# The chunked recurrence of one RWKV mixer: two summands stacked on the partitions, and Gram products with K and B as one weight

## The chip, the core and the metric

The kernel runs on one core of a Trainium2 chip. A core has engines that each work through a queue of their own in order: TensorE (PE in the profile; its weight loads are PEld) multiplies matrices into the accumulation memory PSUM, VectorE (DVE) and ScalarE (ACT) work on rows of 128 partitions, GpSimd (POOL) is a general engine, and SyncE (SP) issues the transfers (DMAs) between the off-chip memory and the on-chip buffer. Semaphores make an engine wait for another. The metric is the time of one execution on the chip in microseconds (us), less is better.

## The reference

The whole program is two transformer blocks over 1024 positions of width 1024. The change is inside the first block's RWKV branch. Per head (8 heads of 64) and direction (forward and reversed) it runs this recurrence over the 1024 positions:

```python
def step(state, inp):
    r_t, w_t, k_t, v_t, a_t, b_t = inp
    sa = jnp.einsum('bhvk,bhk->bhv', state, a_t)
    state = (state * w_t[:, :, None, :] + sa[..., None] * b_t[:, :, None, :]
             + v_t[..., None] * k_t[:, :, None, :])
    return state, jnp.einsum('bhvk,bhk->bhv', state, r_t)
y_f = wkv7_scan(r_h, decay_h[:, :, 0], k_dir[:, :, 0], v_h, -kk, kk * a_h[:, :, 0])
y_b = fl(wkv7_scan(fl(r_h), fl(decay_h[:, :, 1]), fl(k_dir[:, :, 1]), fl(v_h),
                   fl(-kk), fl(kk * a_h[:, :, 1])))
```

`w` (decay) and `a` come from small products of rank 64 (LORA). Beside it stands an attention branch (MLA, 8 heads); both are gated, multiplied by a branch matrix and by `w_out`, and go into a mixture of experts. The second block (windowed attention, a gated linear recurrence, experts) follows. Everything but the first block's mixer is left as it is.

## The kernel before

The recurrence is computed in chunks of CH = 64 positions (NCH = 16 of them) and in fp32, of which each matmul is two records of PE. A pair p of heads (four pairs) lies on the two halves of the 128 partitions, one head on each; both directions (u or d, 0 and 1) lie side by side in the columns.

`phase_a` makes the input projection z tile by tile (matmuls of three split terms, L286 to L288). Its hook `after` starts the RWKV work as the tiles of a pair are done. `prep` (four times for a pair: two halves g of the sequence, two directions d) makes, for eight chunks at once, the decayed keys K and B, the rows A and R (`rAR`), and from them by `gram` (L552) the four triangular 64x64 products of a chunk. There K and B are laid as block-diagonal weights (`diag`, L609 and L610) so that one matmul of 128 rows gives both heads. `flip` (L530) transposes four of the factors. All nine factors of a chunk go by DMA to `P.rw` in device memory, in one layout of 128 partitions. The LORA products at L580 contract over 64 rows, `twd` on one half of the partitions and `ad` on the other, so two of them can lie beside each other. `inverse` inverts the triangular matrices, on DVE for blocks of 32 (L655, L657) and with a few matmuls for the rest (L679, L683).

`rwkv_chain` then goes through the 16 chunks one after the other. For each chunk it has five steps, each a group of matmuls of 64x64 at L742 into the PSUM tile `pc` (two buffers): `ahead` (the two products for the next chunk that don't need the state, copied by ACT to `px`, L761), the main product (copied by DVE to `U`, L779), the state product (added by DVE to the decayed state `SW`, which POOL made at L775, into `S`, L788), and the output `Y` (copied by ACT, L792, and stored). In all it has nine terms for a direction and chunk: two in `ahead`, two in the main product, two for S, three for Y. The factors come back with one DMA for two chunks (`rwt`). `mm` issues the two halves (head 0, head 1) alternately, and an order on PE keeps one accumulation of a half at a time.

The chains of pairs 0 to 2 run inside the projection and the attention; chain 3 runs beside the end of the attention. Attention's steps on PE are scores (L286 to L288, tile `S<-kh,qh`), transposes (L900, `pt`), values (L914, `po`) and sums (L922). `finish` (L693 to L719) normalises a pair's output, and `branch_out` multiplies with the branch matrix (tile `br`), after splitting the inputs by ACT and DVE into two parts (L255: `wlo`, `ol`).

The order of instructions on an engine is no table: when the program is built, a scheduler goes through it with a cost model of its own and lays each engine's instructions in the order of the times that it estimates. So a changed step moves its neighbours, too.

## Time and profile before

| | us |
|---|---|
| median of the runs | 4181.69 (three runs, 4176.91 to 4192.26) |
| the profiled execution | 4153.57, span 4151.8 |
| PE busy | 3737.5 (90% of the span) |
| DVE busy | 2816.6 (68%) |
| ACT busy | 2112.2 (51%) |
| POOL busy | 417.2 (10%) |
| granted PE clock, mean over the span | 0.948 |

The span is the time from the first to the last instruction of the profiled execution. Busy time is the time in which an engine had an instruction at work. The granted clock is the share of full speed that PE was allowed. The rows below are of three kinds: a table of stretches of time with the busy time of each engine, a table of instructions grouped by line and shape, and a timeline of one engine, in which neighbours of one kind are merged.

### The profile page before, as it was taken

The numbers are of one execution on the slowest core, as the hardware profiler recorded it, in microseconds if no ns is written. First come the engines' busy times: TensorE is split into PE (matmuls) and PEld (weight loads), VectorE is DVE, ScalarE is ACT, GpSimd is POOL, SyncE is SP. The second block draws the span as 40 slices with busy tenths as digits, with TensorE's granted clock in tenths as the row PEclk, the third lists the DMA queues.
The fourth block names the chain that finished last, engine by engine and source line by source line (L and its number), as shares of the span: only waits on it lengthen the run. The fifth ranks groups of instructions, "written<-read, shape, count | busy, mean of one in ns | idle before, by whom it ended". The sixth has DMA issues, their size and how long they took to land. (4 is left out here: it accounts for less than half of the span.)

```text
span 4151.8 us, 57961 instructions
## 1 busy us (share of the span) xinstructions
PE 3737.5 (90%) x22538; PEld 2975.9 (72%) x22538; DVE 2816.6 (68%) x4374; ACT 2112.2 (51%) x2621; POOL 417.2 (10%) x313
## 2 busy tenths in 40 slices
PE   7999998999997979996999869999969986999994
PEld 6877776777675766664889757887748875788873
DVE  5556374958756556654366778888867766788887
ACT  4322323443332335554255546777738753677774
POOL 0000000100000014330000011111010000111101
PEclk9999998999998989998999989999979997999997
DMA  3355757563437569984233569999731355999994
GB/s 109 130 165 148 215 166 212 148 191 116 161 109 261 183 241 319 315 272 139 112 97 97 217 261 344 384 383 380 284 127 71 114 191 216 333 379 375 383 372 159
DMA packets 371044, 921.87 MB, mean 222 GB/s; under 512 B 156304, under 2 KB 214416, under 8 KB 298832
## 3 DMA queue, kind: packets, MB, share of 16 engines
q1 hardware_dynamic: 352336, 867.78, 57.9%
q0 software_dynamic: 18432, 50.36, 4.8%
q8 instruction: 178, 2.92, 0.3%
q14 instruction: 98, 0.80, 0.1%
HBM read 767.54 MB, written 167.25 MB: 225 GB/s over the span
## 5 line engine op out<-in xcount | busy, mean ns | idle before, releaser
L255 DVE TENSOR_TENSOR wlo<-wraw,whi 128x2048 fp32r<-128x2048 f32 x498 | 1134.1, 2289 | 297.9 <-ACT whi L255 295.3
L255 ACT ACTIVATE whi<-wraw 128x2048 fp32r<-128x2048 f32 x498 | 955.1, 1919 | 366.8 <-PE g L288 243.0
L287 PE MATMUL g<-wlo,xth 128*128 128x512 f32 x1280 | 509.2, 398 | 5.7 <-DVE wlo L255 5.6
L286 PE MATMUL g<-whi,xth 128*128 128x512 f32 x1280 | 511.4, 400 | 3.2 <-ACT xth L255 2.4
L288 PE MATMUL g<-whi,xtl 128*128 128x512 f32 x1280 | 506.8, 396 | 5.9 <-DVE xtl L255 5.6
L288 PEld LDWEIGHTS g<-whi,xtl 128*128 128x128 f32 x1280 | 242.6, 190 | 62.0 <-DVE xtl L255 10.6
L287 PEld LDWEIGHTS g<-wlo,xth 128*128 128x128 f32 x1280 | 243.1, 190 | 59.4 <-DVE wlo L255 7.9
L286 PEld LDWEIGHTS g<-whi,xth 128*128 128x128 f32 x1280 | 243.2, 190 | 57.3 <-ACT xth L255 4.8
L286 PE MATMUL z<-hT_hi,w_hi 128*128 128x512 f32 x592 | 240.8, 407 | 8.0 <-DVE z_out L402 6.4
L1646 POOL DMA_INDIRECT e_xg<-xm,e_ix x32 | 75.5, 2359 | 1711.2 <-DVE e_ix L1644 952.3
L287 PE MATMUL z<-hT_lo,w_hi 128*128 128x512 f32 x592 | 239.5, 404 | 0.0
L288 PE MATMUL z<-hT_hi,w_lo 128*128 128x512 f32 x592 | 238.3, 403 | 0.0
L287 PE MATMUL g<-wlo,e_hh 128*128 128x512 f32 x512 | 202.4, 398 | 15.2 <-DVE wlo L255 15.2
L286 PE MATMUL g<-whi,e_hh 128*128 128x512 f32 x512 | 204.4, 400 | 8.2 <-ACT e_hh L255 8.0
L288 PE MATMUL g<-whi,e_hl 128*128 128x512 f32 x512 | 196.5, 391 | 0.2
L775 POOL TENSOR_SCALAR SW<-S,wc 128x64 f32<-128x64 f32 x120 | 67.2, 575 | 773.6 <-DVE S L788 440.3
L286 PEld LDWEIGHTS z<-hT_hi,w_hi 128*128 128x128 f32 x592 | 113.3, 191 | 38.5 <-DVE z_out L402 6.6
L288 PEld LDWEIGHTS z<-hT_hi,w_lo 128*128 128x128 f32 x592 | 112.8, 191 | 31.6 <-issue 6.1
L287 PEld LDWEIGHTS z<-hT_lo,w_hi 128*128 128x128 f32 x592 | 113.5, 192 | 27.5 <-issue 2.3
L1246 PE MATMUL g<-wraw,m_hT 128*128 128x512 f32 x256 | 117.3, 598 | 13.6 <-ACT m_y L1247 6.8
L287 PEld LDWEIGHTS g<-wlo,e_hh 128*128 128x128 f32 x512 | 96.4, 188 | 42.9 <-DVE wlo L255 24.9
L286 PEld LDWEIGHTS g<-whi,e_hh 128*128 128x128 f32 x512 | 96.3, 188 | 32.9 <-ACT e_hh L255 14.4
(522 smaller groups left out, 8040.9 us busy)
## 6 DMA issues: line engine op xcount, KB each, us to landing
wraw<-in_w_gu SPq DMA_DIRECT2D x256, 1024.0 KB
wraw<-in_w_dn SPq DMA_DIRECT2D x128, 1024.0 KB
wraw<-in_w SPq DMA_DIRECT2D x96, 1024.0 KB
rwt<-rw SPq DMA_DIRECT2D x32, 1152.0 KB
w_raw<-in_w_in SPq DMA_DIRECT2D x37, 512.0 KB
rw<-flip SPq DMA_DIRECT2D x128, 128.0 KB
gt<-z_out SPq DMA_DIRECT2D x16, 512.0 KB
gate<-gt SPq DMA_DIRECT2D x32, 256.0 KB
```

Of the source, the lines that this page charges most:

```text
L255: return self.nc.scalar.activation(hi, src, AF.Copy), self.nc.vector.tensor_sub(lo, src, hi.bitcast(F32))
L286: t.matmul(ps, lh, rh, start=first, stop=False)
L287: t.matmul(ps, lh, rl, start=False, stop=False)
L288: t.matmul(ps, ll, rh, start=False, stop=last)
L775: nc.gpsimd.tensor_scalar(SW[:, d], S[:, d], P.wc[:, c, 4 * d + p:4 * d + p + 1], None, op0=OP.mult)
L1246: nc.tensor.matmul(ps, ht[:, k], w[:, k, n], start=(k == 0), stop=(k == 1))
L1646: nc.gpsimd.indirect_dma_start(out=xg, out_offset=None, in_=self.x, in_offset=bass.IndirectOffsetOnAxis(ap=ix[:, :1], axis=0))
```

## The change

Two factors whose products are summed anyway are laid above each other on the 128 partitions, so that one matmul of 128 rows makes the sum of both. To allow it, the chunk's tile in device memory gets a new layout (`RW` = 768 columns, `VU`, `XX`, `W2`, `W3`, `LL` and others are column offsets); U is written by the chain into the `rwt` tile under V, and `px`'s part into the tile under X. A chunk and direction has then six terms: two in `ahead` (64 rows), one main product (128 rows), one state product (128 rows), two for the output (one of 64 rows, one of 128). A head's results go to the other half of the partitions where that is needed.

```diff
@@ rwkv_chain
-    def parts(c):
-        if c % 2 == 0:
-            parts.R = pool.tile([128, 2, 1152], F32, name="rwt", bufs=2)
-            nc.sync.dma_start(parts.R, P.rw[p][c // 2])
+    def part(c):
+        R = pool.tile([128, 2, RW], F32, name="rwt", bufs=3)
+        for h, o in enumerate((AN, 0)):
+            nc.sync.dma_start(R[HALF[h], :, o:o + RW - AN], P.rw[p][c][HALF[h], :, o:o + RW - AN])
...
-        mm(ps, lambda u: [(LA[:, u], VT[:, u], 0)] + ([(AN[:, u], XT[:, u], 1)] if c else []))
-        t = pool.tile([128, 2, 2, CH], F32, name="px", bufs=2)
-        nc.scalar.activation(t[:, 0:n], ps[:, 0:128 * n].rearrange("p (x u t) -> p x u t", u=2, t=CH), AF.Copy)
+        t = [(la[h][HALF[h], u], vu[h][HALF[h], u], 1 - h, 64 * u) for u in U2 for h in range(2)]
+        if c:
+            t += [(an[HALF[1 - h], u], xx[h][HALF[1 - h], u], h, 128 + 64 * u) for u in U2 for h in range(2)]
+        mm(ps, t)
+        for h in range(2):
+            nc.scalar.activation(SP[HALF[1 - h], :, h], v(ps)[HALF[1 - h]], AF.Copy)
+            if c:
+                nc.scalar.activation(xx[h][HALF[h]], v(ps, 128)[HALF[h]], AF.Copy)
...
-            for d in U2:
-                nc.gpsimd.tensor_scalar(SW[:, d], S[:, d], P.wc[:, c, 4 * d + p:4 * d + p + 1], None, op0=OP.mult)
+            for h in range(2):
+                s = HALF[h]
+                nc.gpsimd.tensor_mul(SW[s], SP[s, :, h], P.wc[s, c, p:8:4][:, :, None].to_broadcast([64, 2, CH]))
-        mm(ps, lambda u: [(XT[:, u], px[:, 0, u], 0)] + ([(px[:, 1, u], S[:, u], 0)] if S is not None else []))
-        nc.vector.tensor_copy(Ut, v(ps))
+        mm(ps, [(xx[h][both[h], u], SP[both[h], u, h], 1 - h, 64 * u) for u in U2 for h in range(2)])
+        nc.vector.tensor_copy(vu[0][HALF[1]], v(ps)[HALF[1]])
+        nc.vector.tensor_copy(vu[1][HALF[0]], v(ps)[HALF[0]])
...
-            mm(ps, lambda u: [(KT[:, u], VT[:, u], 0), (BT[:, u], Ut[:, u], 0)])
+            mm(ps, [(w2[h][:, u], vu[h][:, u], h, 64 * u) for u in U2 for h in range(2)])
+            for h in range(2):
+                s = HALF[h]
+                if c:
+                    nc.vector.tensor_add(SPn[s, :, h], v(ps)[s], SW[s])
-                nc.vector.tensor_add(Sn, v(ps), SW)
...
-        mm(ps, lambda u: ([(S[:, u], Rr[:, u], 0)] if S is not None else [])
-           + [(VT[:, u], MK[:, u], 0), (Ut[:, u], MB[:, u], 0)])
+        t = [(SP[HALF[h], u, h], rr[HALF[h], u], h, 64 * u) for u in U2 for h in range(2)] if c else []
+        mm(ps, t + [(vu[h][:, u], w3[h][:, u], h, 64 * u) for u in U2 for h in range(2)])
```

In `prep` and `gram`, K and B of one head stand beside each other as one weight of 128 columns over that head's 64 rows. A matmul then gives all four blocks of one head, and the two heads use the two halves of the rows. All products of a group are masked on DVE. LORA products are cut into four of 128 columns, issued alternately.

```diff
@@ gram
-        for g in range(2):
-            ps = self.ps(0)
+        for q in range(2):
+            pm = [self.ps(0) for h in range(2)]
             for c in range(4):
-                nc.tensor.matmul(ps[:, 128 * c:128 * c + 128], lb[:, 4 * g + c], AR[:, :, 4 * g + c], start=True, stop=True)
-            if mask is None:
-                nc.scalar.activation(da[:, cs], v[:, :, 0], AF.Copy)
-            else:
-                nc.vector.tensor_mul(da[:, cs], v[:, :, 0], m(mask))
-            nc.vector.tensor_mul(dr[:, cs], v[:, :, 1], m("m_inc"))
+                for h in range(2):
+                    nc.tensor.matmul(pm[h][:, 128 * c:128 * c + 128],
+                                     KB[HALF[h], 4 * q + c].rearrange("p x t -> p (x t)"),
+                                     AR[HALF[h], :, 4 * q + c], start=True, stop=True)
+            for h in range(2):
+                v = pm[h].rearrange("p (c x t) -> p c x t", x=2, t=CH)
+                nc.vector.tensor_mul(lw[:, :, h], v[:, :, 0], m("m_str"))
+                nc.vector.tensor_mul(lw[:, :, 2 + h], v[:, :, 1], m("m_inc"))
@@ prep
-        for x, act in enumerate((P.twd, P.ad)):
-            nc.tensor.matmul(pm[x], up[rows[x], x], act[rows[x], ts], start=True, stop=True)
+        for q in range(4):
+            for x, act in enumerate((P.twd, P.ad)):
+                o = ts.start + 128 * q
+                nc.tensor.matmul(pm[x][:, 128 * q:128 * q + 128], up[rows[x], x], act[rows[x], o:o + 128],
+                                 start=True, stop=True)
```

The stores of the factors (`put`, `pairs`), the loads of `inverse` and the order of `flip`'s copies follow the new layout.

The scheduler lays the changed work anew. At three places it reads as follows. In the new kernel's listing the same steps have other line numbers: chain matmuls L759 (for L742), Gram products L555 (for L552), LORA products L585 (for L580), attention's transposes L926, values L940 and sums L948 (for L900, L914, L922), the U copies L801 and L802 (for L779), the state's additions L811 (for L788).

First, PE where attention ends and chain 3 goes on, before:

```order
L742 MATMUL pc<-rwt 64x64 x4
L900 MATMUL pt<-cst,p 128x128 x4
L914 MATMUL po<-pts,V 64x128 x8
L742 MATMUL pc<-rwt,U 64x64 x4
L914 MATMUL po<-pts,V 64x128 x7
L922 MATMUL po<-cst,m 64x128 x2
L695 MATMUL pc<-y_8353,cstb 128x512
```

And now:

```order
L940 MATMUL po<-pts,V 64x128 x7
L948 MATMUL po<-cst,m 64x128 x2
L759 MATMUL pc<-rwt 64x64 x4
L759 MATMUL pc<-rwt,SP 64x64 x4
L759 MATMUL pc<-rwt 64x64 x4
L514 MATMUL pc<-cst,hbc 128x128 x4
L759 MATMUL pc<-rwt 64x64 x8
L759 MATMUL pc<-SP,rwt 64x64 x4
L737 MATMUL pc<-r,cstb 128x512
L759 MATMUL pc<-rwt 64x64 x4
```

The last group of the chain stood ahead of attention's last; now eight more chunks stand behind it, 200 chain matmuls, with 30 matmuls of the branch product and some of `finish` among them.

Second, DVE at the same place, where before the last copies of the chain and of attention stood next to each other:

```order
L788 TENSOR_TENSOR S<-pc,SW 128x128
L926 TENSOR_TENSOR ot<-ot,po 128x128
L904 COPY pts<-pt 128x512
L779 COPY U<-pc 128x128
L926 TENSOR_TENSOR ot<-ot,po 128x128
```

And now:

```order
L801 COPY rwt<-pc 64x2x64
L802 COPY rwt<-pc 64x2x64
L811 TENSOR_TENSOR SP<-pc,SW 64x2x64 x2
L255 TENSOR_TENSOR wlo<-wraw,whi 128x2048
L801 COPY rwt<-pc 64x2x64
L802 COPY rwt<-pc 64x2x64
L255 TENSOR_TENSOR wlo<-wraw,whi 128x2048
L255 TENSOR_TENSOR ol<-oraw,oh 128x512 x3
L811 TENSOR_TENSOR SP<-pc,SW 64x2x64 x2
```

Each copy and each addition of a chunk is now two instructions on half of the partitions, and pieces of the branch product's split stand among them, which came behind the chain before.

Third, PE at the Gram products, where the number of the tile tells the half (a tile for each head, on its own half of the rows). Before, four of one tile on the whole array follow four of another:

```order
L552 MATMUL pw_1277<-rAR_1258,bd0_199 128x128 x4
L552 MATMUL pw_1284<-rAR_1258,bd0_199 128x128 x4
```

Now, in a place where they alternate, and in one where they don't:

```order
L555 MATMUL pw_1276<-rAR_1258,rKB_1266 128x128 x2
L555 MATMUL pw_1277<-rAR_1258,rKB_1266 128x128 x2
L555 MATMUL pw_1276<-rAR_1258,rKB_1266 128x128
L555 MATMUL pw_1277<-rAR_1258,rKB_1266 128x128
L555 MATMUL pw_1276<-rAR_1258,rKB_1266 128x128
L555 MATMUL pw_1277<-rAR_1258,rKB_1266 128x128
```

```order
L555 MATMUL pw_1530<-rAR_1512,rKB_1520 128x128 x4
L555 MATMUL pw_1531<-rAR_1512,rKB_1520 128x128 x4
```

The program's order is one head, then the other, throughout; the scheduler keeps it for part of the groups only. Over the whole stage 133 of the 256 Gram matmuls have the other head's as neighbour and 123 one of their own.

## Rows read from the trace of the kernel before

**Rows 1.** The page's first line: the span and the count of instructions.
```profile
span 4151.8 us, 57961 instructions
```

**Rows 2.** Stretches: start:end, length, busy PE PEld DVE ACT POOL, clock, DMA share, GB/s.
```profile
0.00:1247.00 1247.00, 1158.95 (x9970) 898.45 (x9972) 774.13 (x1736) 431.24 (x817) 78.23 (x141) 0.96 0.52 156
1200.00:1247.00 47.00, 47.00 (x718) 37.96 (x717) 19.03 (x42) 18.25 (x40) 5.15 (x12) 1.00 0.19 66
1247.00:1270.00 23.00, 9.58 (x38) 6.23 (x35) 12.30 (x28) 8.03 (x11) 0.00 (x0) 0.60 0.86 316
```

**Rows 3.** The same table for the instructions of L742 alone: PE, PEld.
```profile
0.00:1247.00 1247.00, 175.21 (x4448) 148.44 (x4448) 0.96 0.52 156
```

**Rows 4.** Table by line, 0 to 1300: count, busy us, mean ns, idle before, its releaser.
```profile
L742 PE MATMUL pc<-rwt 64*64 64x64 f32 x1984 | 94.3, 225 | 10.4 <-DVE S L788 5.1 <-DMA rwt<-rw 3.4 <-ACT Y L792 1.9
...
L742 PE MATMUL pc<-px,rwt 64*64 64x64 f32 x512 | 29.4, 235 | 4.7 <-ACT px L761 4.7
...
L742 PE MATMUL pc<-U,rwt 64*64 64x64 f32 x480 | 27.1, 232 | 5.2 <-DVE U L779 3.2 <-DVE m L890 2.0
...
L742 PE MATMUL pc<-rwt,U 64*64 64x64 f32 x512 | 26.4, 223 | 2.0 <-DVE m L890 2.0
```

**Rows 5.** Timeline of PE at the stage's end: start us, length us, instruction, count.
```profile
1229.16 0.45 PE L742 MATMUL pc<-px,rwt 64*64 64x64 f32 x8
1229.44 0.40 PE L742 MATMUL pc<-S,px 64*64 64x64 f32 x8
1229.68 0.40 PE L742 MATMUL pc<-rwt 64*64 64x64 f32 x8
1230.01 0.66 PE L900 MATMUL pt<-cst,p 128*128 128x128 f32 x4
...
1246.41 0.45 PE L742 MATMUL pc<-rwt,U 64*64 64x64 f32 x8
1246.79 0.98 PE L914 MATMUL po<-pts,V 128*64 128x128 f32 x13
1247.50 0.27 PE L922 MATMUL po<-cst,m 128*64 128x128 f32 x1
...
1252.96 2.04 PE L695 MATMUL pc<-y,cstb 128*128 128x512 f32 x2 [4.86 <-DVE y L693]
```

**Rows 6.** The same timeline at two adjacent LORA products.
```profile
251.82 0.69 PE L580 MATMUL pw<-twd,lora_up 64*128 64x512 f32 x1
251.83 0.69 PE L580 MATMUL pw<-ad,lora_up 64*128 64x512 f32 x1
252.35 0.59 PE L580 MATMUL pw<-twd,lora_up 64*128 64x512 f32 x1
...
252.88 0.50 PE L286 MATMUL z<-hT_hi,w_hi 128*128 128x512 f32 x1
```

**Rows 7.** The same timeline at eight Gram products.
```profile
920.40 2.05 PE L552 MATMUL pw<-rAR,bd 128*128 128x128 f32 x16
922.21 0.48 PE L286 MATMUL S<-kh,qh 128*128 128x512 f32 x1
```

**Rows 8.** Table by line again: DVE's and ACT's pieces.
```profile
L609 DVE TENSOR_TENSOR bd<-t,t 64x512 f32<-64x512 f32 x32 | 21.9, 683 | 0.2
...
L761 ACT ACTIVATE px<-pc 128x256 f32<-128x256 f32 x60 | 23.0, 383 | 68.2 <-PE pc L742 68.1
...
L779 DVE COPY U<-pc 128x128 f32<-128x128 f32 x64 | 18.2, 285 | 37.3 <-PE pc L742 36.9
...
L792 ACT ACTIVATE Y<-pc 128x128 f32<-128x128 f32 x64 | 17.5, 274 | 60.6 <-PE pc L742 60.4
...
L788 DVE TENSOR_TENSOR S<-pc,SW 128x128 f32<-128x128 f32 x56 | 16.0, 285 | 27.3 <-PE pc L742 26.9
...
L255 DVE TENSOR_TENSOR wlo<-wraw,whi 128x2048 fp32r<-128x2048 f32 x5 | 11.4, 2290 | 1.1 <-ACT whi L255 1.0
```

**Rows 9.** Table by line again: GpSimd's scaling of the state.
```profile
L775 POOL TENSOR_SCALAR SW<-S,wc 128x64 f32<-128x64 f32 x120 | 67.2, 575 | 773.6 <-DVE S L788 440.3 <-DVE S L786 212.4 <-DVE m L890 74.2
```

More of the change, by code (lines that the diff above doesn't have):

```diff
@@ L225, in keep @@
         self.gt = [dram.tile([128, T], F32, name=f"gt{j}") for j in range(16)]
-        self.rw = [dram.tile([8, 128, 2, 1152], F32, name=f"rw{p}") for p in range(4)]
+        self.rw = [dram.tile([NCH, 128, 2, RW], F32, name=f"rw{p}") for p in range(4)]
         self.kn = [dram.tile([128, T], F32, name=f"kn{j}") for j in range(4)]
@@ L728, in rwkv_chain @@
     U2 = range(2)
[L729 removed]
     pst = lambda: psum.tile([128, 512], F32, name="pc", bufs=2)
[L731 to L732 removed]
+    v = lambda ps, o=0: ps[:, o:o + 128].rearrange("p (u t) -> p u t", t=CH)
     def mm(ps, terms):
         last = [None, None]
[L737 to L746 removed]
@@ L764, in rwkv_chain @@
-    S = None
-    q = parts(0)
-    px = ahead(0, q)
+        for l, r, half, o in terms:
+            i = nc.tensor.matmul(ps[HALF[half], o:o + 64], l, r, start=last[half] is None, stop=True,
+                                 skip_group_check=True)
+            if last[half] is not None:
+                P.order(i, last[half])
+            last[half] = i
+    def part(c):
+        R = pool.tile([128, 2, RW], F32, name="rwt", bufs=3)
+        for h, o in enumerate((AN, 0)):
+            nc.sync.dma_start(R[HALF[h], :, o:o + RW - AN], P.rw[p][c][HALF[h], :, o:o + RW - AN])
+        one = lambda m: R[:, :, m:m + CH]
+        two = lambda *m: [one(x) for x in m]
+        return (one(AN), one(RR), two(LL, LL + CH), two(W2, W2 + CH), two(W3, W3 + CH), two(*VU), two(*XX))
@@ L767, in rwkv_chain @@
+    new = lambda: pool.tile([128, 2, 2, CH], F32, name="SP", bufs=3)
+    q, SP = part(0), new()
+    ahead(0, q, SP)
     for c in range(NCH):
-        _, Rr, _, MB, MK, BT, KT, VT, XT = q
+        _, rr, _, w2, w3, vu, xx = q
         if c % 2 == 0:
```

145 lines of the change are left out of this document (68 added, 77 removed).

## The prediction

> **What bounds the kernel now.** I read the page's first section for the whole, then the table of stretches, then the table by line of the stage that the diff touches, then the timeline at three places. The profiled run has a span of 4151.8 us [rows 1]. The edit sits in the first 1247 us, the stage of projection, RWKV preparation, four chains and attention (MLA); after it the orders of the two kernels are practically the same, so I let everything later stand. In that stage TensorE (PE) is busy for 1158.95 of 1247 us, VectorE (DVE) for 774, ScalarE (ACT) for 431, GpSimd (POOL) for 78, the DMA engines for 0.52 of their time; in its last 47 us PE is busy without a gap [rows 2]. So PE sets the pace, and an edit is worth what it takes off PE's queue, as long as no wait comes back. PE sits idle for 88 us of the stage; only 22.3 of them end in a chain matmul (10.4 + 4.7 + 5.2 + 2.0, [rows 4]). Chain 3 and attention end side by side: the chain's last group starts at 1246.41, attention's last products at 1247.50 [rows 5]. Then comes the latency of `finish(3)`: PE idles 4.86 us before the matmul at 1252.96 [rows 5].
>
> **Chain matmuls (six terms for nine).** The trace has 4448 records on L742, two for each fp32 matmul, so 2224 matmuls [rows 3]; the order of the changed kernel has 1488. A group of four matmuls (8 records, two on each half of the array) starts 0.24 us before the next (1229.44 to 1229.68, [rows 5]), which is 0.06 each: 2224 x 0.06 = 133 us, 1488 x 0.06 = 89. Of the new ones 736 contract over 128 rows and write 64 of the columns, so two still lie side by side, if this pairing holds for 64 columns of data as for the rest (a rival, below). 70 neighbours in the new order stand on the same half and can't overlap: + 70 x 0.06 = 4. Sum: 93 - 133 = **-40 us**, all on PE's queue.
>
> **Gram products.** 256 matmuls of 128 columns before and after. Before, 8 of them (16 records) take 1.81 us (920.40 to 922.21, [rows 7]), 0.226 each, 58 us in all. After, each contracts over 64 rows and the heads lie on two row halves. That row halves overlap shows in the LORA products: the two start 0.01 us apart, the second half of the first one 0.53 later, and the next z matmul starts 1.06 after the first, the time of one of them alone [rows 6]. But in the new order only 133 of the 256 stand next to the other half; 123 follow one of their own half (four and four is common). With 0.113 for a matmul and 0.113 more for each such neighbour, 256 x 0.113 + 123 x 0.113 = 43 us, some 45 with the ends of runs: **-13 us**.
>
> **LORA products.** Cut in four and meant to alternate. They overlap already where they stand side by side [rows 6], and in 13 of 16 preparations the new order has four of one and then four of the other: **0**.
>
> **Changes of array size on PE.** Going from 64x64 to another shape and back costs time: the first group of a visit takes 0.28 (1229.16 to 1229.44), the middle one 0.24, the last 0.33 (1229.68 to 1230.01, [rows 5]). So 0.04 at entry, 0.09 at exit, 0.13 for a change. Up to the end of the last chain the order has 554 changes of array size before and 704 after, since the state products now switch within the chain between 128 and 64 rows, and the Gram products have become 64 rows high among 128-row neighbours: 150 x 0.13 = **+20 us**. This is half of what the chain saves. The bounds are 0 (the drain is hidden in weight loads) and 150 x 0.18 = 27 (the exit's 0.09 twice).
>
> The Trainium skill speaks against this change at that very point: "TensorEngine Tiling (Array Packing)", section Tiling Modes, Key Properties, says that a change of the mode, not merely of the tile, drains TensorE. The trace agrees, with the 0.13 us just read; if changes were free, the sum below would be -26 where it is now -6.
>
> PE's queue therefore gets shorter by 40 + 13 - 20 = 33 us. Against that stand the waits.
>
> **What DVE, ACT and POOL get.** A half copy of 64 partitions does not cost half: 64x512 on DVE takes 683 ns where 128x128 takes 285, so time goes by the elements of a partition and not by partitions [rows 8]. The U copy at L779 becomes two (64 to 128) and the S addition at L788 becomes two (60 to 120); at 0.285 that is +18 and +17 us, and 32 more masked Gram copies, which I estimate at 0.43 between those two sizes, are +14: DVE +49 of 774. ACT gets 248 small copies at 0.274 (L792's) in place of 64 at 0.383 [rows 8]: +44, less 12 for 32 Gram copies of px's size that leave it. Neither becomes the bound, both have over 400 us free. But each of the new copies stands in an in-order queue behind attention's reductions and exponentials, and PE waits for the last of two rather than for one. If the 22.3 us of idle time before chain matmuls [rows 4] grow by half, **+10 us**; bounds 0 (attention's matmuls cover it all) and 22 (they double).
> POOL: 120 multiplications of 575 ns become 112 that take two directions at once [rows 9]. POOL is busy 78 of 1247 us [rows 2]; two at 0.575 run beside main product, U copy and S product (0.45 + 0.57 + 0.45), so **0**; should the new form take 2 us, the eight chunks below would pay 0.5 us each.
> SP: the load of a pair of chunks (32 of 1152 KB) becomes four loads of half the partitions, 128 in all, and some 50 more stores are issued. PE waited once for such a load, 3.4 us [rows 4], and the DMA engines are at 0.52 [rows 2]. **0**, bounds -3 and +6.
>
> **The tail.** Here the order moves something the diff doesn't tell: the last attention matmul now stands before the last eight chunks of chain 3, where before both ended together. Behind it PE has 200 chain matmuls (12 us), 30 matmuls of the branch product, a few of `finish` and the changes of size between them, some 27 us by the prices above. A chunk is a serial loop: main product 0.45, two U copies 0.57, S product 0.45, two additions 0.57, then the products for the next chunk 0.68, whose buffer comes free with the additions, and four ACT copies 1.10. This is 3.8 us with nothing between; before, with one copy where two are now, 2.5. DVE has three split pieces of 2.29 [rows 8] and seven of about 0.68 in between, 11.6 us; if three quarters stand in the way, 1.1 per chunk. 8 x 4.9 = 39 us, 27 of work, so **+12 us** idle; bounds 6 (chunks of 4.1) and 29 (chunks of 7).
> With idle time comes a lower clock: in the 23 us after 1247, with PE busy for 9.58, the granted clock is 0.60, while it is 1.00 in the full stretch ahead [rows 2]. If a fifth of the tail's work runs at 1.2 GHz and not at 2.4 GHz, **+5 us** (0 to 10).
>
> **Sum.** -40 - 13 + 20 + 10 + 12 + 5 = -6 us. The profiled run of before took 4153.57 us, span 4151.8, so the same run after would take 4148. The median of the runs shown is 4181.69, 28 us above the profiled one; on it the forecast is 4176, **no change**. A measurement of this kernel can tell about 0.5%, 21 us, from no change.
>
> **Rivals.**
> 1. *Faster: the extra copies hide.* PE has attention's matmuls to run while the chain waits, the chain's own waits shrink with its shorter products (say 8 of the 22.3 us go), and the tail costs only its lower bound of 6: -33 - 8 + 6 = -35, which gives 4147. For it speaks that PE alone is full; against it that the last eight chunks stand behind attention, with no such work left.
> 2. *Slower: the tail is a row of latencies.* Place: the eight chunks behind attention's last matmul. If a chunk takes 8.5 rather than 4.9 us, because U copies, additions and ACT copies stand behind split pieces of 2.29 us and the clock stays at 1.2 GHz, then + 8 x 3.6 = 29, and the sum is +23: 4205. It decides from chunks of about 8.3 us. For it: every link stands in an in-order queue that also carries the branch product's split pieces; against it: those on DVE come to 11.6 us in all.
> 3. *The change doesn't do what it says:* 128x64 products with 64 columns of data don't overlap. Then 736 x 0.06 = 44 us come back: +38, 4220. For it: no row here has such a pair with 64 columns. Against it: attention's products of that shape with 128 columns do overlap, 13 records in 0.71 us (1246.79 to 1247.50, [rows 5]), 0.055 each, half of the 0.113 of a Gram record on the whole array [rows 7].
>
> **How the numbers follow.** Forecast 0.43, faster rival 0.34, slower rival 0.17, no overlap 0.06. So faster by over 0.5% has 0.34, within 0.5% 0.43, slower 0.23. The range goes from 4128 (the faster rival with changes of size at their lower bound) to 4220 (the third rival); beyond these I leave about 0.1 at each end. The forecast's own range is 4161 to 4202.
>
> **What would show it.** In the profile after: 2976 records on the chain's line with steps of 0.24 for each group of four matmuls, also in the 128-row ones (if 0.48, rival 3); groups of eight Gram matmuls at 0.9 to 1.6; about 0.13 us at each change; PE busy in the stage at about 1126 us; a stretch of some 39 us between attention's last matmul and the chain's last, with PE idle for 12. A tail over 66 us would mean rival 2; no gap in it, rival 1. I am wrong altogether if the time moves after the end of the branch product, where the order is unchanged.

## The result and the profile after

The changed kernel takes 4226.34 us in the median (4220.48 to 4230.18, four runs) against 4179.30 us of the kernel before (four runs): a ratio of 1.0121, with a 95% interval of 1.0104 to 1.0138. It is slower, by 47 us, where no change was forecast. Each later run has a base of its own; "by the ratio" below means that its ratio to that base is what is compared.

The profiled run of before, 4153.57 us, turned out to lie below all timed runs of that kernel (4160 to 4192). So below its second profile stands for it (e12, span 4170.3 us, time 4172.12). The span after is 58 us longer than that, more than the 47 us of the medians, since the profiled run after, 4230.18 us, is the longest of its four.

The page's first line after answers [rows 1]:

```profile
span 4228.4 us, 56033 instructions
```

The table of stretches, of before (second profile) up to attention's last products; columns as in [rows 2]:

```profile
0.00:1262.00 1262.00, 1172.44 (x9976) 908.23 (x9978) 774.54 (x1736) 432.15 (x817) 78.04 (x141) 0.95 0.52 154
```

The same of the changed kernel, to attention's last products and from there to the chain's end:

```profile
0.00:1271.00 1271.00, 1158.90 (x8303) 898.93 (x8303) 813.10 (x1853) 449.62 (x960) 55.51 (x117) 0.92 0.55 151
1271.00:1332.00 61.00, 44.31 (x437) 30.98 (x433) 27.39 (x54) 20.60 (x52) 8.00 (x14) 0.71 0.85 235
```

Up to attention's end PE was busy 14 us less, but attention's end came 9 us later (1271 for 1262): PE idled for 112 us where it had idled for 90, at a granted clock of 0.92 for 0.95. Then follow 61 us in which chain 3 goes on, beside the first work of the branch product, PE busy for 44 of them at a clock of 0.71. Before, this stretch didn't exist.

The lower clock has one main place, 600 to 800 us, before (second profile) and after:

```profile
600.00:800.00 200.00, 170.65 (x1801) 130.49 (x1801) 120.61 (x268) 67.01 (x139) 20.08 (x32) 0.87 0.70 199
```

```profile
600.00:800.00 200.00, 165.41 (x1371) 127.61 (x1367) 127.12 (x266) 70.43 (x175) 14.06 (x29) 0.74 0.67 176
```

There PE idled 5 us more, at a clock of 0.74 for 0.87. The same stretch has 0.74 to 0.82 in all ten profiles of whole kernels with the six-term chain, and 0.85 to 0.93 in all eight with the old one (0.87 with the new Gram products alone, e1 below; 0.93 with the doubled copies alone, e5). So the lower clock came with the new chain; which part of it brings it, no run here shows.

The chain's matmuls, to 1340 us (after the stretch and its length: PE's busy time and records), of before, second profile:

```profile
0.00:1340.00 1340.00, 177.89 (x4448) 151.01 (x4448) 0.95 0.53 161
```

and after, which answers [rows 3]:

```profile
0.00:1340.00 1340.00, 185.79 (x2976) 143.64 (x2976) 0.91 0.56 155
```

A third of the records is gone, as counted, and PE was busy with the rest 8 us longer than with all of them before. One reason shows in the timeline after, at full clock, at attention's end (columns as in [rows 5]):

```profile
1269.56 0.40 PE L759 MATMUL pc<-SP,rwt 128*64 128x64 f32 x8
1269.79 0.93 PE L940 MATMUL po<-pts,V 128*64 128x128 f32 x13
...
1271.21 0.45 PE L759 MATMUL pc<-rwt,SP 64*64 64x64 f32 x8
1271.59 0.45 PE L759 MATMUL pc<-rwt 128*64 128x64 f32 x8
1271.97 0.66 PE L514 MATMUL pc<-cst,hbc 128*128 128x128 f32 x4
...
1330.97 0.83 PE L759 MATMUL pc<-rwt 128*64 128x64 f32 x8
1337.82 2.05 PE L717 MATMUL pc<-y,cstb 128*128 128x512 f32 x2 [6.03 <-DVE y L715]
```

Four matmuls on 128 rows and 64 columns take 0.23 us (1269.56 to 1269.79): column halves overlap. But a group that stands alone between others of another shape takes 0.38 (1271.21 to 1271.59, 1271.59 to 1271.97). Of the new chain's 372 groups 179 stand so and 138 in pairs; before, nearly all of the 556 stood two to four together. The last two rows are the end: chain 3's last group at 1330.97, and 6.03 us of idle time before `finish(3)`, where it was 4.86 [rows 5].

The Gram products, in a group of four and four and in an alternating one; this answers [rows 7]:

```profile
394.97 1.85 PE L555 MATMUL pw<-rAR,rKB 64*128 64x128 f32 x16 [0.92 <-DVE rKB L619]
396.74 0.50 PE L286 MATMUL z<-hT_hi,w_hi 128*128 128x512 f32 x1
...
402.07 1.17 PE L555 MATMUL pw<-rAR,rKB 64*128 64x128 f32 x16
403.17 0.50 PE L287 MATMUL z<-hT_lo,w_hi 128*128 128x512 f32 x1
```

From the start of eight matmuls to the next work it is 1.77 us in the first place and 1.10 in the second, where it was 1.81.

The engines beside PE, by line (columns as in [rows 4]); this answers [rows 8] and [rows 9]:

```profile
L798 POOL TENSOR_TENSOR SW<-SP,wc 64x128 f32<-64x128 f32 x112 | 54.2, 483 | 806.6 <-DVE SP L811 515.9 <-DVE SP L813 286.5
...
L781 ACT ACTIVATE SP<-pc 64x128 f32<-64x128 f32 x128 | 34.0, 266 | 101.6 <-PE pc L759 100.7
...
L811 DVE TENSOR_TENSOR SP<-pc,SW 64x128 f32<-64x128 f32 x112 | 32.0, 285 | 28.9 <-PE pc L759 26.9
...
L801 DVE COPY rwt<-pc 64x128 f32<-64x128 f32 x64 | 18.8, 294 | 46.4 <-PE pc L759 45.0
```

All copies on half of the partitions cost what full ones did, and the new form of the state's scaling is no slower.

### The profile page after: what moved, and what is told of

Same layout as the page of the kernel before. It is cut to its first block, busy times and chain, and to the rows that moved or that the text cites. A ratio compares the mean times of both kernels' runs of the same rounds, so it can differ in the third digit from the quotient of the medians.

```text
span 4228.4 us, 56033 instructions
## 1 busy us (share of the span) xinstructions
PE 3779.7 (89%) x21258; PEld 3005.3 (71%) x21258; DVE 2870.4 (68%) x4530; ACT 2141.2 (51%) x2805; POOL 400.0 (9%) x303
## 5 line engine op out<-in xcount | busy, mean ns | idle before, releaser
L759 PE MATMUL pc<-rwt 64*64 64x64 f32 (+1 forms) x1984 | 119.0, 252 | 21.4 <-DVE rwt L801 11.4
L759 PEld LDWEIGHTS pc<-rwt 64*64 64x64 f32 (+1 forms) x1984 | 90.8, 155 | 61.4 <-issue 19.3
L798 POOL TENSOR_TENSOR SW<-SP,wc 64x128 f32<-64x128 f32 x112 | 54.2, 483 | 806.6 <-DVE SP L811 515.9
```

The source lines that it names most:

```text
L759: i = nc.tensor.matmul(ps[HALF[half], o:o + 64], l, r, start=last[half] is None, stop=True, skip_group_check=True)
L798: nc.gpsimd.tensor_mul(SW[s], SP[s, :, h], P.wc[s, c, p:8:4][:, :, None].to_broadcast([64, 2, CH]))
```

## Experiments

The first question was whether the loss sits in the chain or in the preparation, and whether it needs attention at all. **Theory A**: the RWKV branch's own serial path (preparations, inverse, chain 3) has become the later of two ends, and the change makes that path longer. **Theory B**: the chunks' doubled copies cost it all, as in the prediction's slower rival.

### Parts of the change

e1: before with the new `gram` and LORA; the stores of the Gram products are cut in halves, eight for a preparation where there were four.

```diff
-        B = self.diag(0, lambda o, s: nc.vector.tensor_mul(o, ta3[s], iW3[s]))
-        K = self.diag(1, lambda o, s: nc.vector.tensor_mul(o, kd3[s], iW3[s]))
+        KB = pool.tile([128, NH, 2, CH], F32, name="rKB", bufs=1)
...
+        self.gram(p, d, g, KB, AR)
```

> The kernel before with only the preparation changed: K and B as one weight, heads on row halves, LORA products in four pieces; the chain keeps its nine terms and its layout, and some stores are cut in two halves. Theory A (the RWKV branch's own serial path, preparations to inverse to chain, now sets the stage's end, and the new preparation lengthens it): slower, by 20 to 50 us, since the built order already lays chain 3 from attention step 53 on, where it was 46, and 236 of its matmuls behind attention. Theory B (the loss is all in the chain's doubled copies): the chain is as before, so within 10 us of before, or faster by up to 13.

Measured: 4184.75 us, ratio 1.0036 (1.0021 to 1.005), 15 us slower by the ratio, 10 by the medians (base 4174.55). This lies between the two theories' numbers (20 to 50, or at most 10) and decides nothing.

e2: the changed kernel with the old block-diagonal `gram` and whole LORA products.

```diff
-        self.gram(p, d, g, KB, AR)
+        LT, MB = self.t3("rLT", "l"), self.t3("rMB")
+        self.gram(B, AR, LT, None, MB)
+        for h in range(2):
+            self.put(p, d, NH * g, HALF[1 - h], LL + 64 * h, LT[HALF[h]])
...
```

> The changed kernel with the preparation of before: block-diagonal Gram weights, LORA products whole; the chain has six terms, and the Gram stores are cut in halves for the new layout. Theory A (the serial path of the RWKV branch sets the end, and each part of the change lengthens some of it): slower than before by 10 to 40 us, less than both parts together; chain 3 begins at attention step 52 in the built order. Theory B (the loss is all in the chain's doubled copies): the full loss of the change, 40 to 50 us.

Measured: 4215.45 us, ratio 1.0099 (1.0082 to 1.0116), 41 us slower. The number lies at the edge between the theories (10 to 40, and 40 to 50), so it doesn't decide between them either. The chain with its layout carries most of the loss, the preparation some: 41 and 15 by the ratios, where both together cost 51.

### The RWKV path without attention

e3 and e4: attention left out of either kernel.

```diff
+    zero = pool.tile([128, T], F32, name="zero", bufs=1)
+    nc.vector.memset(zero, 0.0)
+    for j in range(4):
+        nc.sync.dma_start(P.om[j], zero)
+    return
```

> The kernel before with attention left out (its output is set to zero), so that the RWKV branch runs on free engines after the projection. One look for the length of the RWKV path by itself, beside the same cut of the changed kernel. Theory A: the last chain ends at some 1000 to 1100 us, close to the 1247 of the whole kernel. Theory B: well before 900, since a path with that much slack can't set the end.

> The changed kernel with attention left out (its output is set to zero). Theory A: the RWKV path by itself is longer than in the same cut of before, by 30 to 80 us at the end of chain 3, most of it between a preparation and the inverse after it. Theory B (chain copies): preparations and inverses at the same distances as before, only chunks longer, by 1 us each.

Measured, one run each: 4028.12 and 4107.43 us, 79 us apart, more than the 47 of the whole kernels. The first instruction of the fourth inverse on DVE, and the chain's last group on PE, of e3:

```profile
920.95 0.16 DVE L655 TENSOR_TENSOR rXp<-rX,rLd 128x1 f32<-128x1 f32 x1 [5.53 <-DMA rLd<-rL]
...
1115.39 0.45 PE L742 MATMUL pc<-rwt,U 64*64 64x64 f32 x8
```

and of e4:

```profile
990.74 0.16 DVE L676 TENSOR_TENSOR rXp<-rX,rLd 128x1 f32<-128x1 f32 x1 [5.24 <-DMA rLd<-rw]
...
1209.78 0.89 PE L759 MATMUL pc<-rwt 128*64 128x64 f32 x8
```

Without attention the chain ends at 1115 before and at 1210 after. Of these 94 us (1115.39 to 1209.78), more than the 30 to 80 that were expected, 70 are there when the fourth inverse starts (920.95 and 990.74); the inverse itself and the steps to the chain are alike (113 us in both); the last 24 are chain 3's own (82 us before, 106 after, from its first to its last group). So theory A holds in its main point: the path is longer without attention, too, and most of that lies ahead of the inverse. The clock is not alike in the two runs, though: 0.77 and 0.59 at 600 to 800 us, 0.88 and 0.66 while chain 3 runs. So the 24 us can't be put down to the copies of theory B, and how much of the 70 is clock isn't shown.

### The doubled copies alone

e5: before, with U copies, S additions and `px` copies cut in halves.

```diff
-        nc.vector.tensor_copy(Ut, v(ps))
+        for x in h2:
+            nc.vector.tensor_copy(Ut[x], v(ps)[x])
...
-                nc.vector.tensor_add(Sn, v(ps), SW)
+                for x in h2:
+                    nc.vector.tensor_add(Sn[x], v(ps)[x], SW[x])
```

> The kernel before with the chain's copies and additions cut in halves as in the changed kernel (two U copies, two S additions, four ACT copies in ahead), nine terms as before. Theory A (the RWKV path sets the end; a chunk's loop grows by 0.29 + 0.29 + 0.7 us): chain 3 longer by 20 us when run beside little else, so slower by 5 to 20 us. If the loop's copies hide behind attention: within 5 us.

Measured: 4171.97 us, ratio 0.9997 (0.9983 to 1.0011). In the nine-term kernel the doubled copies cost nothing in time, with an order in which the fourth inverse comes 29 us earlier and attention ends 12 us later than before. e15 turned it round: the changed kernel with the copies shared between DVE and ACT.

```diff
-            nc.scalar.activation(SP[HALF[1 - h], :, h], v(ps)[HALF[1 - h]], AF.Copy)
+            (nc.vector.tensor_copy if h else lambda o, i: nc.scalar.activation(o, i, AF.Copy))(SP[HALF[1 - h], :, h], v(ps)[HALF[1 - h]])
...
-        nc.vector.tensor_copy(vu[1][HALF[0]], v(ps)[HALF[0]])
+        nc.scalar.activation(vu[1][HALF[0]], v(ps)[HALF[0]], AF.Copy)
```

> The changed kernel with the chain's half copies shared between two engines: one of the two U copies on ACT, and half of ahead's state copies on DVE, so that a chunk's loop is shorter by 0.3 to 0.8 us. If the loop of the chunks behind attention decides (the slower rival of the prediction): some 50 us of exposed chain shrink by 5 to 13 us. If the delay in the preparations decides: within 5 us, the exposed stretch just starts as late.

Measured: 4229.45 us, ratio 1.0135 (1.0109 to 1.0162): nothing gained. Theory B falls as the explanation of the whole loss.

### What holds up the preparations

The fourth inverse needs the triangular Gram product of the last preparation (`LT` before, a part of `rLW` after): stored to device memory, loaded again by four DMAs (`rLd`). This is SP's queue there, before (second profile; the start, the time to issue all of a row's DMAs, and what they move):

```profile
954.56 0.32 SPq L632 DMA_DIRECT2D rL<-rLT  x1
...
958.02 0.52 SPq L648 DMA_DIRECT2D rLd<-rL  x1
958.64 3.80 SPq L535 DMA_DIRECT2D rw<-flip  x4
962.48 1.48 SPq L648 DMA_DIRECT2D rLd<-rL  x3
```

and after:

```profile
1025.22 0.54 SPq L497 DMA_DIRECT2D rw<-rLW  x1
1028.13 1.93 SPq L543 DMA_DIRECT2D rw<-flip  x3
1030.35 1.19 SPq L768 DMA_DIRECT2D rwt<-rw  x2
1031.58 6.06 SPq L543 DMA_DIRECT2D rw<-flip  x8
1037.75 0.55 SPq L768 DMA_DIRECT2D rwt<-rw  x1
1038.40 1.01 SPq L821 DMA_DIRECT2D yd<-Y  x2
1039.46 0.55 SPq L768 DMA_DIRECT2D rwt<-rw  x1
1040.05 0.61 SPq L543 DMA_DIRECT2D rw<-flip  x1
1040.70 2.23 SPq L669 DMA_DIRECT2D rLd<-rw  x4
```

Before, `LT` is ready after the first of two Gram products, one store of 0.32 us goes out (954.56), and the loads follow at 958.02 and 962.48, with four stores of transposed factors between them. After, the last masked product goes out at 1025.22, when all Gram products are done, and then twelve stores of transposed factors (`rw<-flip`, 8.6 us in all), four loads of the chain and two stores of its output issue before the loads at 1040.70: 15.5 us from store to load, where the last three loads before left 7.9 us after the store. At this place alone the loads are some 8 us later (from the store to the end of the last load's issue, 9.4 us before and 17.7 after). SP works its queue in the order in which it was built.

The delay adds up over the four pairs. From the scan on DVE in a pair's last preparation to the start of its inverse it is 24, 31, 23 and 30 us before (29 for the last in the first profile), and 33, 33, 45 and 46 after: 49 us more in all, of the 80 by which the fourth inverse starts later (966.54 and 1046.55). The other 31 lie between an inverse and the last scan of the next pair, and no run separates them.

"DMA: Bandwidth & Descriptors" of the Trainium skill, section Anatomy of one DMA (SWDGE, gpsimd path), which describes DMAs that GpSimd issues, says that the DMA engines don't wait on semaphores; a wait is served on the issuing sequencer ahead of the dispatch. This case's trace agrees for SP: its queue waited 13 times, 14.9 us in all, for ACT's copies ahead of these stores (300 to 1250 us of the changed kernel), and the loads stood behind them.

So three remedies were tried. e6 takes the chain's loads (128 in place of 32) out of SP's queue; e7 and e8 let the scheduler place the inverse's loads first, in the changed kernel and in the one before; e13 and e14 take the stores of the transposed factors out of SP's queue, in either kernel.

```diff
-            nc.sync.dma_start(R[HALF[h], :, o:o + RW - AN], P.rw[p][c][HALF[h], :, o:o + RW - AN])
+            nc.gpsimd.dma_start(R[HALF[h], :, o:o + RW - AN], P.rw[p][c][HALF[h], :, o:o + RW - AN])
```

> The changed kernel with the chain's loads (two for a chunk) issued from GpSimd's queue and not from SP's. Theory A with SP's queue as the link (the loads take 0.74 us of SP each, 1.5 us for a chunk where it was 0.2, and stand ahead of the preparation's stores and the inverse's loads): faster than the changed kernel by 10 to 30 us, the fourth inverse starts earlier by as much. If SP is not the link: within 8 us of the changed kernel.

Measured: 4222.77 us, ratio 1.0118 (1.0092 to 1.0143). No gain by the ratio; the chain's loads as such are not the link.

```diff
-        for u in units:
-            for h, b in part:
-                nc.sync.dma_start(Ld[at(u, h, b)], self.low(p, u, h, 32 * b, 32 * b))
+        with P.tc.high_priority():
+            for u in units:
+                for h, b in part:
+                    nc.sync.dma_start(Ld[at(u, h, b)], self.low(p, u, h, 32 * b, 32 * b))
```

> The changed kernel with the sixteen loads at the start of each inverse given precedence in the scheduler, so that they don't stand behind the transposed factors' stores in SP's queue. Theory A: each inverse starts some 5 to 14 us sooner after its preparation, the time is 10 to 25 us below the changed kernel. If these loads aren't on the path that sets the end: within 8 us.

Measured: 4200.37 us, ratio 1.0061 (1.004 to 1.0083), 25 us below the changed kernel by the ratio.

> The same precedence in the kernel before. Theory A says that the RWKV path nearly set the end there too: faster by 3 to 15 us. If PE's work sets the end there: within 3 us.

Measured: 4158.83 us, ratio 0.996 (0.9949 to 0.9971): 16 us faster than before.

```diff
-            self.P.nc.sync.dma_start(self.P.rw[p][NH * g + c:NH * g + NH:2, HALF[half], d, o:o + w]
+            self.P.nc.gpsimd.dma_start(self.P.rw[p][NH * g + c:NH * g + NH:2, HALF[half], d, o:o + w]
```

> The changed kernel with the stores of the transposed factors (twelve for a preparation, some 0.65 us of SP's queue each) issued from GpSimd's queue. If the inverse's loads are late because they stand behind these stores in SP's queue: the third and fourth inverse start 10 to 25 us earlier and the time falls by 10 to 30 us. If the gain of the run with precedence was luck of that built order: within 8 us of the changed kernel.

Measured: 4207.22 us, ratio 1.0082 (1.0059 to 1.0105), 16 us less by the ratio. SP's queue of this run at the same place:

```profile
1002.82 0.39 SPq L497 DMA_DIRECT2D rw<-rLW  x1
1007.24 1.55 SPq L669 DMA_DIRECT2D rLd<-rw  x4
```

From the last product's store to the loads it is now 4.4 us (1002.82 to 1007.24) and no longer 15.5. The fourth inverse starts at 1012 in place of 1047. The distances from scan to inverse are 34, 34, 36 and 31 us, so about half of the 49 us is gone.

> The same stores (eight for a preparation) from GpSimd's queue in the kernel before. If SP's queue is on the path there too: faster than before by 5 to 20 us, as the run with precedence; if not: within 5 us.

Measured: 4150.19 us, ratio 0.9951 (0.9934 to 0.9967), 20 us faster than before by the ratio. The stores ahead of the inverse's loads are a link of the path in both kernels.

### The Gram products and their buffers

A preparation has two PSUM buffers for all its products. Before, a Gram product, two transposes, the other Gram product and two transposes took turns in them; after, the products of two heads take both at a time, and the transposes come behind all four groups. Without attention (e3, e4) the preparations 10 to 13 of 16 came 27 to 29 us after one another before, and 32 to 35 after. e9 issues the old interleaving.

```diff
-        self.gram(p, d, g, KB, AR)
+        self.gram(p, d, g, KB, AR, 0)
...
             self.pairs(p, d, g, 1 - h, AN, t[:, :, h])
+        self.gram(p, d, g, KB, AR, 1)
```

> The changed kernel with a preparation's work issued in the old interleaving: first half of the Gram products, the transposes of A, second half of the Gram products, the other transposes. Theory A, second part (the Gram products of two heads take both PSUM buffers of the preparation, so that no transpose runs beside them and each preparation lasts some 6 us longer): preparations follow each other 3 to 6 us sooner, the fourth inverse starts 15 to 40 us earlier, the time is 8 to 30 us below the changed kernel. If that spacing isn't on the path: within 8 us.

Measured: 4215.77 us, ratio 1.0097 (1.0077 to 1.0118), some 10 us less, which is not clear of noise: the interval overlaps the changed kernel's. The inverse starts at 1028, 19 earlier, but the preparations don't follow each other sooner (10 to 13 take 118 us, 120 in the changed kernel), as they should by the explanation with the buffers; 14 of the 19 us lie between the last scan and the inverse. With precedence for the inverse's loads:

> The same with precedence for the inverse's loads as well. Theory A: both gains add up at least in part, 30 to 50 us below the changed kernel, that is 4175 to 4195, near the kernel before. If one of them was luck of the built order: 4200 or more.

Measured: 4225.18 us, ratio 1.0119 (1.0102 to 1.0136). That is the loss in full: the two remedies don't add up, so the gain of e7 hangs at least in part on the order that came out there. With the stores on GpSimd's queue and the interleaving:

> The changed kernel with the old interleaving of Gram products and transposes and with the transposed factors' stores on GpSimd's queue. Over the runs so far the time follows the start of the fourth inverse about one for one. If the two causes (PSUM buffers held by the Gram products, stores ahead of the inverse's loads in SP's queue) are apart, the fourth inverse starts at 985 to 1005 and the time is 25 to 45 us below the changed kernel; if they are one slack gained twice, 1010 to 1030 and 10 to 20 us.

Measured: 4197.82 us, ratio 1.006 (1.004 to 1.008), 25 us below the changed kernel by the ratio; the inverse starts at 1027, though, and not before 1005, and the distances from scan to inverse add up to 152 us, hardly less than the changed kernel's 157. Half of the loss is still there. What the interleaving brought in the three runs that have it is 10 us (e9), a loss of 24 beside e7 (e10) and 9 beside e13 (e17): that the Gram products' hold on the buffers is a cause of its own is not shown.

### PE's share, and the size of an order's luck

e11: before with two of the three terms of the chain's output left out.

```diff
-        mm(ps, lambda u: ([(S[:, u], Rr[:, u], 0)] if S is not None else [])
-           + [(VT[:, u], MK[:, u], 0), (Ut[:, u], MB[:, u], 0)])
+        mm(ps, lambda u: [(Ut[:, u], MB[:, u], 0)])
```

> The kernel before with two of the three terms of the chain's output left out (the output is wrong by them): 496 chain matmuls fewer, 30 us by 0.06 us each, none of them in the loop that carries the state from chunk to chunk. The prediction's reading (PE's queue sets the end): faster by 20 to 30 us. Theory A (the RWKV path sets the end as soon as PE is relieved): faster by less than 12 us.

Measured: 4143.39 us, ratio 0.9923 (0.9906 to 0.9939), 30 us faster. The prediction's reading (20 to 30) has its number, and theory A in its plain form is refuted here: PE work taken away outside the loop of the RWKV path is worth its full price, and both ends come earlier (chain 3's at 1228 in place of 1261, attention's at 1220 in place of 1262). e12 and e16 are the controls.

> The kernel before once more, unchanged, for a second profile of it: the first profiled run lies at the lower end of its times. Attention's last products and chain 3's end are expected some 10 to 25 us later than in the first profile, at 1257 to 1272, with the rest after them as long as there.

Measured: 4172.12 us; chain 3's last group at 1261, attention's last products at 1262, both 15 us later than in the first profile.

> The changed kernel with the LORA products whole, as before. They overlap in either form, so the prediction's term for them is 0: within 5 us of the changed kernel by that term; a change of more than 10 us would show how far the built order alone moves the time, since only the order changes much (chain 3 from attention step 49 on, not 55, and 104 chain matmuls behind attention, not 200).

Measured: 4213.58 us, ratio 1.0113 (1.0083 to 1.0142), by the ratio the loss but for 3 us, with an order that lays chain 3 quite elsewhere.

e18 put both remedies on the kernel before.

> The kernel before with both remedies, the stores on GpSimd's queue and the precedence of the inverse's loads: a candidate that beats both kernels. If the RWKV path is still the later end: 25 to 35 us below before. If attention's end has become the later one: no more than the 20 us of the stores alone.

Measured: 4142.46 us, ratio 0.992 (0.9889 to 0.9951): 33 us faster than before, and the fastest of the kernels here that compute the whole.

### One table

Times in us from each run's trace: the start of the fourth inverse on DVE, chain 3's last group and attention's last products on PE, the span, and the span less the later of the two ends.

| run | 4th inverse | chain 3's last | attention's last | span | rest |
|---|---|---|---|---|---|
| before, second profile (e12) | 967 | 1261 | 1262 | 4170 | 2908 |
| after | 1047 | 1331 | 1271 | 4228 | 2897 |
| e1, preparation alone | 1000 | 1274 | 1237 | 4177 | 2904 |
| e2, chain alone | 1022 | 1318 | 1269 | 4216 | 2898 |
| e5, before, copies cut | 938 | 1239 | 1275 | 4178 | 2903 |
| e6, chain's loads on GpSimd | 1037 | 1326 | 1259 | 4218 | 2892 |
| e7, loads first | 1013 | 1295 | 1249 | 4190 | 2895 |
| e8, before, loads first | 958 | 1247 | 1266 | 4161 | 2895 |
| e9, interleaved | 1028 | 1324 | 1279 | 4218 | 2894 |
| e10, e9 with e7 | 1025 | 1319 | 1266 | 4223 | 2904 |
| e11, before, less PE work | 957 | 1228 | 1220 | 4141 | 2913 |
| e13, stores on GpSimd | 1012 | 1307 | 1258 | 4205 | 2899 |
| e14, before, stores on GpSimd | 943 | 1233 | 1252 | 4148 | 2897 |
| e15, copies shared | 1042 | 1339 | 1261 | 4234 | 2895 |
| e16, LORA whole | 1026 | 1319 | 1291 | 4212 | 2893 |
| e17, e9 with e13 | 1027 | 1304 | 1250 | 4196 | 2892 |
| e18, before, both remedies | 941 | 1236 | 1241 | 4140 | 2899 |

The last column stays between 2892 and 2913, while the span moves by 94: the time follows the later of the two ends. The 21 us of that column are as much as some of the gains above, so the gains rest on the times of the runs and not on this table. In every kernel with the six-term chain or the new Gram products chain 3 is the later one; in the variants of before attention is, or the two ends are within 8 us. The two ends are not independent: in e11 both come earlier, by 33 and 42 us. And one trace says little of a few microseconds: the two profiles of the kernel before are 7 us apart at the fourth inverse and 15 at both ends.

## Why the prediction was wrong

- **What bounds the kernel.** "So PE sets the pace" was half of it. PE's work does set attention's end, and e11 returns 30 us for 30. But the two ends stood level in the very rows that the prediction quoted (1246.41 and 1247.50, [rows 5]); the RWKV branch was a second path with no slack, and the sum had no line for it. This is the step that failed: everything that the change adds between a preparation and its inverse was priced as engine time that has room, not as delay on a path that has none. The fourth inverse starts 80 us later, chain 3 ends 70 us later. In the sum's own terms, attention's end should have come some 50 us earlier (33 off PE's queue and 27 of work moved behind it, less 10 of waits) and came 9 later, and the tail behind it should have lasted 44 us and lasted 60: of the 75 us that the chain's end was missed by, 59 lie ahead of attention's end. A second step failed beside it, the clock (below).
- **SP, priced at 0 (-3 to +6).** Wrong. Moving stores out of its queue gives 16 us in the changed kernel and 20 in the one before (e13, e14). The prediction looked at the DMA engines' share of 0.52 and at one wait of PE; the queue's order was the thing, and PE doesn't wait for it directly.
- **Gram products, -13.** PE was busy 66.5 us with them where it was 71.4, 5 us less and not 13. The overlap was right (1.10 for 1.81 where heads alternate), but the step is no gain: e1, with the stores that the new form needs, is 10 to 15 us slower.
- **Chain matmuls, -40, and changes of array size, +20.** Counts and prices hold: 0.23 for a group, 0.38 where the shape changes. But PE's busy time on these lines went from 177.89 to 185.79, at a lower clock over the stretch (0.91 for 0.95) and with most groups now bordering on another shape; the two shares weren't separated.
- **LORA, 0.** Not contradicted: 3 us by the ratio between e16 and the changed kernel, within both intervals.
- **Doubled copies, +10.** e5 shows 0 in the nine-term kernel. Waits did come: idle time ahead of attention's end rose by 22 us.
- **The tail, +12 of idle time in 39 us.** The eight chunks are there, and last 60 us (1270.78 to 1330.97), 7.5 each where 4.9 was forecast and 8.3 was the slower rival's point. PE idles 17 us in it, 5 more than forecast; the rest of the excess is its work, 44 us busy for 27 by the prices. A chunk at full clock (1.00 from 1309.02 to 1313.03), from one main product to the next, and then one at half clock (0.50):

```profile
1309.02 0.61 PE L759 MATMUL pc<-SP,rwt 128*64 128x64 f32 x8
...
1313.03 0.89 PE L759 MATMUL pc<-SP,rwt 128*64 128x64 f32 x8 [0.76 <-ACT rwt L783]
...
1323.08 0.27 ACT L781 ACTIVATE SP<-pc 64x128 f32<-64x128 f32 x1 [2.87 <-PE pc L759]
1323.38 0.27 ACT L783 ACTIVATE rwt<-pc 64x128 f32<-64x128 f32 x1
...
1323.70 1.13 PE L759 MATMUL pc<-SP,rwt 128*64 128x64 f32 x8 [0.76 <-ACT rwt L783]
...
1323.83 0.27 ACT L783 ACTIVATE rwt<-pc 64x128 f32<-64x128 f32 x1
1324.88 0.29 DVE L801 COPY rwt<-pc 64x128 f32<-64x128 f32 x1 [5.51 <-PE pc L759]
1325.20 0.28 DVE L802 COPY rwt<-pc 64x128 f32<-64x128 f32 x1
...
1325.22 1.00 PE L759 MATMUL pc<-rwt 128*64 128x64 f32 x8 [0.39 <-DVE rwt L801]
...
1326.16 0.69 PE L759 MATMUL pc<-rwt,SP 64*64 64x64 f32 x8
...
1326.33 0.61 DVE L811 TENSOR_TENSOR SP<-pc,SW 64x128 f32<-64x128 f32 x2 [0.85 <-PE pc L759]
...
1328.66 0.27 ACT L781 ACTIVATE SP<-pc 64x128 f32<-64x128 f32 x1 [0.81 <-PE pc L759]
```

  The first takes 4.0 us, close to the 3.8 that the prediction had "with nothing between". The second, from `ahead`'s first copy (1323.08) to that of the next chunk (1328.66), takes 5.6 us: the four copies on ACT end at 1324.10, the main product starts after the second of them, PE works at half clock (0.94 for a group at 1325.22, with one change of shape, where 0.38 was read above), and two copies or additions stand between any two products. So the loop was priced right for the full clock; the clock was not. The other 1.9 us up to the mean of 7.5 stand in chunks that wait for the branch product's split or share PE with it, where the forecast had 1.1. The tail is the smaller part of the miss: chain 3 began 88 us later than before (1199 for 1111) and ended 70 later.
- **The clock, +5 (0 to 10), in the tail alone.** Sized too small, and at the wrong place. In the tail the granted clock is 0.71, and PE's 27 us of work took 44. Ahead of attention's end, where the sum had nothing, PE was busy at half clock for 167 us where before for 97 (67 in the first profile); if all of that work took twice its time, this is an estimate of 35 us more than before, as much as PE's queue was to lose. Up to the chain's end PE was busy 1203 us, where about 1126 were forecast. It lies mostly at 600 to 800 us and came with the new chain in every run, so the added waits of 22 us don't explain it by themselves.
- **Not doing what it says.** Refuted: 128x64 products of 64 columns overlap.
- **After the branch product nothing moves.** Not contradicted; what follows the later end is the same within 21 us in all runs. The time fell outside the range, above the third rival's 4220, for a reason that none of the three rivals had; the slower one had the right place for 16 of the 75 us.

**What is left open.** The one cause that is shown is the queue of stores ahead of the inverse's loads; taking it away returns 16 of the 51 us by the ratio (e13). With the interleaving 25 are back (e17), and what the interleaving does is open. e2 has the old Gram order and is still 41 us slower; its third inverse starts 50 us after the scan of the preparation ahead of it, where before it is 23, with the last four loads issued one by one over 20 us, between other stores:

```profile
774.39 0.48 SPq L678 DMA_DIRECT2D rLd<-rw  x1
...
784.10 5.27 SPq L544 DMA_DIRECT2D rw<-flip  x8
789.42 0.50 SPq L678 DMA_DIRECT2D rLd<-rw  x1
...
794.50 0.36 SPq L678 DMA_DIRECT2D rLd<-rw  x1
```

So the same stores stand ahead of its loads, but no run took them away there. Which of its additions (half stores, twelve stores for eight, loads in four pieces) carries that delay was not separated, nor what in the new chain lowers the clock at 600 to 800 us. An even cut of the chain's tile with one load for a chunk was not tried.

## What to carry to other kernels

When two chains of work end together in a profile, price the change on both, also where one is made of waits and small DMAs that no busy share shows. Follow the data from a producer's store to the consumer's load through the issuing queue, since a store added for another consumer can stand between them. Work removed from the busiest engine is worth its time only if nothing is added to the path beside it and its clock stays; here a change that cut a third of the chain's matmuls brought 47 us of loss, and another queue for some stores with precedence for some loads in the old kernel 33 us of gain.

## What the runs showed of the hardware

A group of four fp32 matmuls of 64 columns took 0.38 us at full clock between groups of another array shape, and 0.23 beside its own: 0.15 for the change, 0.13 by the prediction's rows. Two 128x64 fp32 products of 64 columns run side by side: a group took 0.23 us, as one of 64x64 did (0.24, [rows 5]). An addition on 64 partitions took VectorE 285 ns, as long as one on 128 ([rows 8]). GpSimd's queue issued the strided stores of the transposed factors in 0.63 us each, hardly faster than SP: 0.72 at the place shown (8.6 us for twelve), 0.66 on the mean of the changed kernel's 192. The row of e13, GpSimd by line, 300 to 1100 us (third and fourth number: busy us, mean ns of one):

```profile
L543 POOL DMA_DIRECT2D rw<-flip x156 | 97.0, 629 | 123.3 <-ACT flip L630 121.5 <-issue 1.7
```
